# Output projection by seven block products, with the sums of its left operand added by transfers within SBUF

## The chip, the cores and the metric

The kernel runs on one core of a Trainium2 chip. The metric is the time of one execution on the device in microseconds (us); of the kernel before three runs were taken: 902.49, 902.62 and 902.78 us, median 902.62. The engines are named as in the profile: PE (TensorE, the matrix unit), DVE (VectorE), ACT (ScalarE), POOL (GpSimd) and SP (SyncE, which here only issues transfers).

## The reference

One layer of a hybrid backbone: 512 latent tokens and 256 context tokens of width 1024, all arithmetic in float32. What the change touches is the output projection of the token mixer, the residual and the second norm behind it:

```python
merged = sigmoid(ga) * (a @ w_br_a) + sigmoid(gb) * (ob @ w_br_b)   # 512 x 1024
y_x    = merged @ w_o                                              # 512 x 1024 x 1024
x      = x + g1x * y_x
hx2    = rms_norm(x, norm2_g) * (1 + sc2x) + sh2x
x      = x + g2x * conv_ffn(hx2, ...)       # up to 2 x 2816, 3x3 depthwise conv, gelu, down to 1024
```

`g1x`, `sh2x`, `sc2x` and `g2x` are slices of `silu(c) @ w_ada + b_ada`.

## The kernel before

**Products in float32.** Each operand of a large product is split into two float32r tiles: `hi` is the cast on ACT, `lo` the rest by a subtraction on DVE. A product is three matmuls, hi·hi, hi·lo and lo·hi (L423, L441, L1382).

**Weights.** All weights pass as tiles of 128 x 1024 numbers (512 KB) through one list, `specs`. `stream_load` (L250) issues a tile's transfer on SP's queue into one of five `raw` buffers, `stream_split` (L260) makes `wh` on ACT (L277) and `wl` on DVE (L278), five of each, and `weights()` (L300) hands out the next tile, splits two ahead and loads four more ahead.

**Stages, in order of time.** Projections of q, k, v, u with the gated linear attention of four heads between them (to about 248 us); then five products of 512 x 1024 x 1024, for r, vs, ga, gb and w_br_a, each by `gate` (L1387); then w_br_b and w_o by `wide_tm` (L444); the second norm; the up-projection with the convolution (22 pairs of tiles, to 790 us); the down-projection.

**Seven block products.** `gate` and the down-projection split tokens, inner dimension and columns in halves and form the four blocks of a product from seven block products instead of eight (Winograd's form of Strassen's scheme). A block product of a gate is 24 matmuls of 128x128 by 512 columns (`gate_product`, L1373). Sums of quarters of the weights are made in HBM by POOL's transfers, with an add in the transfer where there is a second summand (`sums_build`, L230). Such a transfer is issued behind a certain matmul (`behind_pe`, L106); each call of `weights()` advances the list of these transfers, those of the gates from the first tile on, those of the down-projection from tile `SUMS0` = 90 on. Sums of the left operand are made by DVE.

**The output projection before.** `wide_tm` takes all eight products: per column half and token tile t, 24 matmuls. In the first half the weights are the outer loop, in the second the token tiles. `mg_turn` (L1580) turns one 128-column slice of `merged` by four 128x128 transposes on PE and splits it: four of the eight slices inside the product with w_br_b, four inside that with w_o, by `hook`.

**The gate columns.** `ada2` (L1192) makes four slices of the conditioning in the background, one step per `tick`. At its end a product with a matrix of ones spreads each of four rows over all partitions; for `sh` and `sc` DVE multiplies it with the identity (L1231) and reduces it (L1235), which gives them as columns.

**Behind the output projection.** `wo_add` (L1664) multiplies with `g1` and adds the residual, ACT squares and sums (L1668), `norm2_root` and `norm2_scale` scale a token tile, `norm2_turn` (L1640) turns two token tiles by 16 transposes, and `norm2_out` (L1652) applies `sh` and `sc` on ACT and splits. `turn_first` (L1672) does so for tokens 0 to 255; it stands 27 matmuls before the end of the output projection. The first tile of the up-projection then starts with the columns of these 256 tokens (24 matmuls of 256 columns, and 16 of the second tile), before the other 256 tokens are turned.

**What sets the order.** A scheduler sets the order of each engine's queue, except where `in_order` (L94) or `behind_last` (L391) fix it; from `turn_first` to the first tile of the up-projection the order of PE, ACT and DVE is the order of the code. Within an engine's queue nothing overtakes.

## Time and profile before

| | |
|---|---|
| time, median of three runs | 902.62 us |
| the profiled execution | 904.17 us, its span 902.4 us |
| PE busy | 887.0 us (98%), 4440 matmuls |
| DVE busy | 742.1 us (82%) |
| ACT busy | 482.4 us (53%) |
| POOL busy | 85.3 us (9%) |
| granted clock of PE | 0.997 of full speed |

A page of the profile shows one execution. A matmul's row is longer than its share of the time, since the next one starts before it ends; the distance between two starts counts. In the chain of waits (the work that ended last, followed back) each piece has its start, its length and its line, so that a stretch of PE can be read from it directly.

### The profile page before, as it was taken

How to read it: one execution, taken by the hardware profiler on the slowest of the kernel's cores; microseconds unless marked ns; L12 is line 12 of the kernel's file. 1: busy time of each engine (PE TensorE's matmuls, PEld its weight loads, DVE VectorE, ACT ScalarE, POOL GpSimd, SP SyncE). 2: the span in 40 equal slices, each digit the busy share in tenths (PEclk: the TensorE clock that was granted, in tenths of full speed). 3: DMA queues.
4: the chain of work that ended last, by engine and by line, in shares of the span. 5: the costliest groups of instructions: out<-in, count | busy, mean ns of one | idle time of the engine just before them, and what ended most of it. 6: DMA issues, size and time to landing. Idle time of an engine off the chain costs nothing.

```text
span 902.4 us, 12467 instructions
## 1 busy us (share of the span) xinstructions
PE 887.0 (98%) x4440; PEld 739.4 (82%) x4440; DVE 742.1 (82%) x1227; ACT 482.4 (53%) x799; POOL 85.3 (9%) x134
## 2 busy tenths in 40 slices
PE   7999999999999999999999999999999999999996
PEld 5678888988888888888888889888888888888885
DVE  6468777969789899689998658887899987896996
ACT  6256554848676665767433347433443334366663
POOL 1312222321000000000000010001111110000000
PEclk9999999999999999999999999999999999999998
DMA  9984999999268678777994951998999993256552
GB/s 273 349 281 101 299 277 212 233 328 230 72 206 264 192 260 256 244 233 246 388 336 150 308 164 55 283 306 173 195 212 177 182 191 105 89 162 205 174 185 95
DMA packets 155308, 196.12 MB, mean 217 GB/s; under 512 B 9273, under 2 KB 88453, under 8 KB 155245
## 3 DMA queue, kind: packets, MB, share of 16 engines
q1 hardware_dynamic: 131229, 137.39, 48.0%
q0 software_dynamic: 21024, 52.65, 26.3%
q10 hardware_dynamic: 2992, 5.28, 1.6%
q8 instruction: 35, 0.57, 0.2%
q14 instruction: 28, 0.23, 0.1%
HBM read 186.90 MB, written 58.72 MB: 272 GB/s over the span
## 4 chain that ended last, share of the span: by engine, by line
PE 93%; SPq 2%; DMA 2%; DVE 1%; ACT 1%; issue 0%; ACTq 0%
PE mm L423 34%; PE mm L1382 15%; PE mm L441 11%; PE gl L1863 10%; PE gl L1382 6%; PE gl L959 3%; PE mm L1863 2%; DMA wa<-in_w_ada_dram 2%; PE mm L723 1%; PE mm L1071 1%; PE mm L1121 1%; PE gl L441 1%; SPq L333 1%; PE gl L994 1%; PE gl L1251 1%; SPq L354 1%
## 5 line engine op out<-in xcount | busy, mean ns | idle before, releaser
L277 ACT CAST wh<-raw 128x1024 fp32r<-128x1024 f32 x189 | 195.0, 1037 | 181.3 <-PE mm L423 89.9
L278 DVE TENSOR_TENSOR wl<-raw,wh 128x1024 fp32r<-128x1024 f32 x189 | 225.8, 1200 | 46.4 <-ACT wh L277 46.0
L423 PE MATMUL mm<-h2l,wh 128*128 128x512 f32 (+1 forms) x344 | 133.1, 387 | 0.0
L423 PE MATMUL mm<-h2h,wh 128*128 128x512 f32 (+1 forms) x344 | 133.1, 387 | 0.0
L423 PE MATMUL mm<-h2h,wl 128*128 128x512 f32 (+1 forms) x344 | 133.1, 387 | 0.0
L1715 DVE SCALAR_TENSOR_TENSOR cacc<-ca,ccol,cacc 128x441 f32<-128x441 f32 (+2 forms) x176 | 121.9, 695 | 4.4
L423 PEld LDWEIGHTS mm<-h2l,wh 128*128 128x128 f32 x344 | 64.6, 188 | 13.1
L423 PEld LDWEIGHTS mm<-h2h,wl 128*128 128x128 f32 x344 | 64.6, 188 | 13.1
L423 PEld LDWEIGHTS mm<-h2h,wh 128*128 128x128 f32 x344 | 64.6, 188 | 13.1
L1863 PE MATMUL gl<-wl,dah 128*128 128x512 f32 x132 | 51.4, 389 | 0.0
L1863 PE MATMUL gl<-wh,dah 128*128 128x512 f32 x132 | 51.4, 389 | 0.0
L1863 PE MATMUL gl<-wh,dal 128*128 128x512 f32 x132 | 51.4, 389 | 0.0
L236 POOL DMA_DIRECT2D sum<-in_ffn_w_down_dram x24 | 13.2, 554 | 376.0 <-PE mm L441 257.1
L1212 DVE SCALAR_TENSOR_TENSOR acc<-wa,cs,acc 128x512 f32<-128x512 f32 x64 | 46.3, 746 | 0.0
L1716 ACT ACTIVATE cacc<-cacc 128x512 f32<-128x512 f32 x22 | 13.9, 633 | 59.5 <-DVE cacc L1715 59.4
L1382 PE MATMUL mm<-wh,xs 128*128 128x512 f32 x128 | 41.1, 393 | 0.0
L423 PE MATMUL mm<-hxh,wh 128*128 128x512 f32 x104 | 41.0, 394 | 0.0
L423 PE MATMUL mm<-hxl,wh 128*128 128x512 f32 x104 | 40.7, 391 | 0.0
L423 PE MATMUL mm<-hxh,wl 128*128 128x512 f32 x104 | 40.6, 390 | 0.0
L1382 PE MATMUL mm<-wh,hxh 128*128 128x512 f32 x96 | 37.8, 393 | 0.0
L1382 PE MATMUL mm<-wh,hxl 128*128 128x512 f32 x96 | 37.5, 390 | 0.0
L1382 PE MATMUL mm<-wl,hxh 128*128 128x512 f32 x96 | 37.4, 390 | 0.0
(475 smaller groups left out, 2006.6 us busy)
## 6 DMA issues: line engine op xcount, KB each, us to landing
raw<-in_w_in_dram SPq DMA_DIRECT2D x52, 512.0 KB
wa<-in_w_ada_dram SPq DMA_DIRECT2D x96, 256.0 KB
raw<-sum SPq DMA_DIRECT2D x46, 512.0 KB
raw<-in_ffn_w_up_dram SPq DMA_DIRECT2D x44, 512.0 KB
sum<-in_ffn_w_down_dram POOLq DMA_DIRECT2D x30, 512.0 KB, 6.3
sum<-in_w_in_dram POOLq DMA_DIRECT2D x28, 512.0 KB, 8.6
sum<-sum POOLq DMA_DIRECT2D x22, 512.0 KB, 6.9
raw<-in_ffn_w_down_dram SPq DMA_DIRECT2D x15, 512.0 KB
```

What stands on the lines that cost most here:

```text
L236: behind_pe(lambda: G.dma_start(sums[b][dst], ap), G)
L277: A.copy(wh, raw)
L278: V.tensor_tensor(wl, raw, wh.bitcast(F32), op=ALU.subtract)
L333: dma(t_, w_ada[0, kp * nk * P:(kp + 1) * nk * P, c0:c0 + cg].rearrange("(k p) c -> p k c", p=P))
L423: T.matmul(ps, a[:, k, :], b[:, c0:c0 + n], start=(k == 0 and i == 0), stop=(k == KT - 1 and i == 2))
L441: T.matmul(ps, a[:, t * P:(t + 1) * P], b[:, k % 2, :], start=(k == 0 and i == 0), stop=(k == KT - 1 and i == 2))
L959: T.matmul(ps, p_, q_, start=(start and z == 0), stop=(stop and z == 2))
L1212: behind_last(lambda: V.scalar_tensor_tensor(acc[i], coming.pop(0), cs[:, k, 0:1], acc[i], op0=ALU.mult, op1=ALU.add), V)
L1382: T.matmul(banks[t], a(kk, t), w[:, kk, :], start=(first and b == 0 and kk == 0 and i == 0), stop=(b == 1 and kk == 1 and i == 2), skip_gr ...
L1715: V.scalar_tensor_tensor(o, a_[:, r0 + dy:r1 + dy, c0 + dx:c1 + dx], wcol(tap), o, op0=ALU.mult, op1=ALU.add)
L1716: A.activation(acc, acc, AF.Gelu)
L1863: T.matmul(ps, a, w[:, kk, :], start=(first and kk == 0 and i == 0), stop=(last and kk == n_ - 1 and i == 2), skip_group_check=True)
```

## The change

The product with w_o is taken by seven block products. In detail:

- `w_o` becomes a sixth entry of `gate_weights`: eight sums of two blocks of its quarters are built in HBM by 16 more transfers on POOL's queue, behind those of w_br_a. Its tiles in `specs` are 14 instead of 8, in the order `WO_ORDER` = (0, 3, 1, 2, 5, 4, 6).
- `m_turn` turns a block of `merged` (a11, a12, a21, a22, for each half b of the inner dimension) by four transposes; six of the eight blocks now lie inside the product with w_br_b, two in the first block product. Of the left sums p1, s2, q4, s3 for b = 0, 1, six additions are made by POOL's transfers from one SBUF tile into another with an add (`m_add`), two on DVE; `m_pair` splits them.
- Results leave in another order: column half 0 of tokens 0 to 255, column half 1 of them, then column half 1 of tokens 256 to 511, then column half 0 of those. The two token tiles of a half are normed together. `turn_first` stands behind the first six matmuls of the last block product. PE's order is fixed for the whole stage.
- `sh` and `sc`: ACT copies row 0 of each of the four products with ones and writes it to HBM (`col_rows`, 16 rows of 128), SP reads the 16 rows back, PE turns them, DVE copies the columns.
- The sums of the down-projection begin at tile 106 instead of 90, with one more step at every fourth tile.
- Four of the eight normalisations of `vs` go from DVE to ACT.

```diff
-SUMS0 = 90
+SUMS0 = 106
...
+WO_ORDER = (0, 3, 1, 2, 5, 4, 6)
...
-gate_weights.append((quarters(w_br_a[0], 0), sum_tiles(2)))
+gate_weights += [(quarters(w_[0], 0), sum_tiles(2)) for w_ in (w_br_a, w_o)]
...
-            for _ in range((i >= at and (at > 1 or i < R_AT or gate_pace(i))) + (at <= i < DENSE)):
+            for _ in range((i >= at and (at > 1 or i < R_AT or gate_pace(i))) + (at <= i < DENSE) + (i >= SUMS0 and at > 1 and i % 4 == 0)):
...
+    def cols_load():
+        rows_c = late([16, P], s="rows")
+        dma(rows_c, col_rows)
+        return lambda: columns(rows_c, 16, "col_both", gl)
...
-                t_ = heap([P, 4, P], s="dg")
-                V.tensor_tensor(t_, ps.rearrange("p (b r) -> p b r", b=4),
-                                ident.unsqueeze(1).to_broadcast([P, 4, P]), op=ALU.mult)
-                if kind not in cols:
-                    cols[kind] = const([P, 8], "col_" + kind)
-                V.reduce_sum(cols[kind][:, j * 4:j * 4 + 4], t_, axis=AX.X)
+                t_ = late([1, 512], s="row")
+                A.copy(t_, ps[0:1, :])
+                adma(col_rows[4 * len(rows_out):4 * len(rows_out) + 4].rearrange("(o b) p -> o (b p)", o=1), t_)
+                rows_out.append(kind)
...
+            if not hf:
+                A.activation(z, z, AF.Identity, bias=shift[:, t:t + 1], scale=var[:, t:t + 1])
...
+    def add(dst, src):
+        G.dma_start(dst, src, accum_op=ALU.add)
...
+    def m_pair(name, b, src, sign):
+        hi, lo = heap([P, 2, 256], F32R, s="mh"), late([P, 2, 256], F32R, s="ml")
+        if sign > 0:
+            A.copy(hi, src)
+            V.tensor_tensor(lo, src, hi.bitcast(F32), op=ALU.subtract)
+        else:
+            A.mul(hi, src, -1.0)
+            V.scalar_tensor_tensor(lo, src, -1.0, hi.bitcast(F32), op0=ALU.mult, op1=ALU.subtract)
+        msum[name, b] = hi, lo
+
+    def m_add(name, b):
+        dst, src = {"p1": ("p1", "a22"), "s2": ("p1", "a11"), "q4": ("p1", "n21"), "s3": ("s3", "a11")}[name]
+        add(mraw[dst, b], mraw[src, b])
...
-    wide_tm(ob, brb_done, brb_step, {(2 + j // 2, 4 * (j % 2)): lambda j=j: mg_turn(j) for j in range(4)})
+    wide_tm(ob, brb_done, brb_step, { (1, 0): lambda: m_do("ta110"), (1, 3): lambda: m_do("ta210", "a110"), (1, 6): lambda: m_do("ta120", "+s30"),
+                                    (2, 1): lambda: m_do("ta220", "+p10"), (2, 4): lambda: m_do("ta111"), (2, 6): lambda: m_do("p10", "+s20"),
+                                    (3, 0): lambda: m_do("ta211"), (3, 2): lambda: m_do("a111", "s20", "+q40"), (3, 6): lambda: None})
...
-    wide_tm(mg, wo_done, hook, {(2, 6): turn_first})
+    WO0 = len(traced())
+    wo_product(0, X, True, {(1, 0): lambda: m_do("ta121", "ta221", "p11")})
+    for t in range(2):
+        A.copy(Y[t], X[t])
+    m_do("s30", "q40", "+s31")
+    ada2_cols()
+    wo_product(3, Y)
+    m_do("s21", "+q41", "a220")
+    squares = [wo_add(0, t, Y[t]) for t in range(2)]
+    wo_product(1, Z, True)
+    m5 = [taken(z) for z in Z]
+    for f in squares:
+        f()
+    wo_product(2, X, False, {(1, 0): lambda: taken_out(0)})
+    taken_out(1)
+    m_do("q41", "s31", "a221")
+    crow_turn(0)
+    behind_last(lambda: A.activation(small(1, "root"), eps_t, AF.Sqrt), A)
+    ada2_end()
+    wo_product(5, Z)
+    for t in range(2):
+        wo_out(1, t, Z[t])
+    scaled(2, 0, 1)
+    crow_turn(1)
+    wo_product(4, X)
+    squares = [wo_add(1, t + 2, combine(m5[t], X[t], ALU.subtract)) for t in range(2)]
+    wo_product(6, X, False, {(0, 1): turn_first})
+    for k2 in (2, 3):
+        norm2_out(0, k2, N2[1][k2], A.copy)
+    for t in range(2):
+        squares[t]()
+        wo_out(0, t + 2, X[t])
+    scaled(2, 2, 3)
+    in_order(WO0, T.engine)
```

Where the order moves. First, ACT's queue around the end of the product with w_br_b; `wh` are casts of weights, `acch` of the conditioning's rows, `mgh` of slices of `merged`. Before:

```order
L415 CAST acch_5232<-acc_4240 128x512
L415 CAST acch_5236<-acc_4243 128x512
L415 CAST acch_5240<-acc_4246 128x512
L415 CAST mgh_5253<-gl_5248 128x512
L277 CAST wh_5354<-raw_5108 128x1024
L277 CAST wh_5409<-raw_5111 128x1024
L415 CAST mgh_5274<-gl_5269 128x512
L277 CAST wh_5457<-raw_5118 128x1024
L277 CAST wh_5488<-raw_5358 128x1024
```

Now, at the same place (`mq` are unsplit blocks of `merged`, `mh` and `ml` their splits; `mh_5277` is p1 of block 0, which one of the new transfers fills):

```order
L1615 COPY mq_5252<-gl_5247 128x512
L1615 COPY mq_5269<-gl_5264 128x512
L1623 ACTIVATE mh_5277<-mq_5223 128x512
L420 CAST acch_5287<-acc_4267 128x512
L282 CAST wh_5410<-raw_5131 128x1024
L420 CAST acch_5291<-acc_4270 128x512
L282 CAST wh_5422<-raw_5133 128x1024
L420 CAST acch_5295<-acc_4273 128x512
L282 CAST wh_5428<-raw_5139 128x1024
L1620 CAST mh_5309<-gl_5303 128x512
L282 CAST wh_5492<-raw_5414 128x1024
```

Ahead of the second w_o tile's cast (`wh_5410`) there now stands a copy that waits for a transfer within SBUF.

Second, ACT's queue behind the first w_o tiles. Before:

```order
L415 CAST mgh_5377<-gl_5372 128x512
L277 CAST wh_5492<-raw_5413 128x1024
L415 CAST mgh_5404<-gl_5399 128x512
L415 CAST mgh_5432<-gl_5427 128x512
L277 CAST wh_5523<-raw_5462 128x1024
L415 CAST mgh_5453<-gl_5448 128x512
L277 CAST wh_5527<-raw_5497 128x1024
L277 CAST wh_5557<-raw_5548 128x1024
L1668 ACTIVATE yt_5531,ss_5332<-x_1209_5310 128x512
```

Now:

```order
L1242 COPY row_5361<-gl_5358 1x512
L1608 ACTIVATE mq_5449<-gl_5444 128x512
L1243 DMA col_rows<-row_5361 1x512
L1608 ACTIVATE mq_5450<-gl_5444 128x512
L1615 COPY mq_5458<-gl_5453 128x512
L1768 COPY mm_5408<-mm_5404 128x512
L1768 COPY mm_5409<-mm_5405 128x512
L1623 ACTIVATE mh_5461<-mq_5449 128x512
L1620 CAST mh_5479<-mq_5224 128x512
L1623 ACTIVATE mh_5483<-mq_5223 128x512
L282 CAST wh_5498<-raw_5426 128x1024
L282 CAST wh_5544<-raw_5490 128x1024
```

Between two casts of weights (`wh_5492`, shown above, and `wh_5498`) there now stand 17 other entries, three of them transfers; `mh_5483` is the split of q4 of block 0, the third sum in a row that a transfer makes in the tile `mq_5223`.

Third, DVE's queue ahead of the up-projection: `yt` and `x` are gate and residual, `xs` the scaled tokens, `h2h` and `h2l` the normed ones split for the up-projection. Before:

```order
L1662 TENSOR_TENSOR h2l_5344<-h2f_5709,h2h_5343 128x256
L1661 CAST h2h_5345<-h2f_5716 128x256
L1662 TENSOR_TENSOR h2l_5346<-h2f_5716,h2h_5345 128x256
L1662 TENSOR_TENSOR h2l_5348<-h2f_5716,h2h_5347 128x256
L1631 TENSOR_REDUCE n2s_5724<-ss_5332 128x1
L475 RECIPROCAL rstd_5726<-rstd_5726 128x1
L1666 TENSOR_TENSOR yt_5757<-mm_5732,g_956_4173 128x512
L1667 TENSOR_TENSOR x_1216_5324<-x_1216_5324,yt_5757 128x512
L1636 TENSOR_SCALAR xs_5760<-x_1213_5318,rstd_5726 128x512
L1631 TENSOR_REDUCE n2s_5765<-ss_5332 128x1
L475 RECIPROCAL rstd_5767<-rstd_5767 128x1
L1636 TENSOR_SCALAR xs_5770<-x_1215_5322,rstd_5767 128x512
```

Now:

```order
L1731 TENSOR_TENSOR h2l_5399<-h2f_5826,h2h_5398 128x256
L1730 CAST h2h_5400<-h2f_5833 128x256
L1731 TENSOR_TENSOR h2l_5401<-h2f_5833,h2h_5400 128x256
L1731 TENSOR_TENSOR h2l_5403<-h2f_5833,h2h_5402 128x256
L1735 TENSOR_TENSOR yt_5841<-mm_5404,g_954_4155 128x512
L1736 TENSOR_TENSOR x_1234_5373<-x_1234_5373,yt_5841 128x512
L1735 TENSOR_TENSOR yt_5846<-mm_5405,g_954_4155 128x512
L1736 TENSOR_TENSOR x_1236_5377<-x_1236_5377,yt_5846 128x512
L1750 TENSOR_REDUCE n2s_5850<-ss_5387 128x2
L480 RECIPROCAL rstd_5852<-rstd_5852 128x2
L1705 TENSOR_SCALAR xs_5855<-x_1234_5373,rstd_5852 128x512
L1705 TENSOR_SCALAR xs_5859<-x_1236_5377,rstd_5852 128x512
```

Before, one token tile's gate and residual (`yt_5757`) stood behind the last split of the first 256 tokens (`h2l_5348`); now two stand there, and both tiles wait for one root.

More of the change, by code (lines that the diff above doesn't have):

```diff
@@ L1385, in backbone_kernel, with gate @@
     banks = []
-    def gate(out, pool, at={}, mids=late, quad=r_quad, sum_=r_sum, pool1=None):
+    def gate(out, pool, at={}, mids=late, quad=r_quad, sum_=r_sum, pool1=None, order=GATE_ORDER, during={}):
         pool1 = pool1 or pool
@@ new lines, in m_turn @@
+    def m_turn(name, b):
+        i, hf = int(name[1]) - 1, int(name[2]) - 1
+        ps = gl()
+        for kk in range(2):
+            for t in range(2):
+                o = (2 * kk + t) * P
+                c0 = (2 * i + kk) * P
+                T.transpose(ps[:, o:o + P], sgb_t[b, 2 * hf + t][:, c0:c0 + P], ident)
+        src = ps.rearrange("p (k t) -> p k t", k=2)
+        raw = lambda: heap([P, 2, 256], s="mq")
+        if name == "a12":
+            z = mraw["p1", b], mraw["s3", b] = raw(), raw()
+            for t_ in z:
+                A.mul(t_, src, -1.0)
+        elif name == "a21":
+            mraw["n21", b] = raw()
+            m_pair(name, b, src, 1)
+            A.mul(mraw["n21", b], src, -1.0)
+        else:
+            mraw[name, b] = raw()
+            A.copy(mraw[name, b], src)
@@ new lines, in m_sum, with m_do @@
+    def m_sum(name, b):
+        if b and name in ("p1", "s2"):
+            dst, src = mraw["p1", b], mraw["a22" if name == "p1" else "a11", b]
+            V.tensor_tensor(dst, dst, src, op=ALU.add)
+        m_pair(name, b, mraw["p1" if name in ("s2", "q4") else name, b], -1 if name in ("p1", "s2", "q4") else 1)
+    def m_do(*what):
+        for w_ in what:
+            if w_[0] == "t":
+                m_turn(w_[1:4], int(w_[4]))
+            elif w_[0] == "+":
+                m_add(w_[1:-1], int(w_[-1]))
+            else:
+                behind_last(lambda: m_sum(w_[:-1], int(w_[-1])), V)
@@ L1697, in backbone_kernel, with scaled, wo_out @@
-    hooks += [(lambda j=j: (mg_turn(j), tick(WT[0])),) for j in range(4, 8)] + [(tick, WT[1])] * 4 + [(ada2_end,)]
-    hooks += [(crow_turn, 0), (crow_turn, 1)]
-    wide_tm(mg, wo_done, hook, {(2, 6): turn_first})
+    def scaled(n, *ts):
+        s_ = small(len(ts), "n2s")
+        V.reduce_sum(s_, ss2[:, ts[0]:ts[-1] + 1, :], axis=AX.X)
+        r = rstd_of(s_, len(ts), D)
+        for t in ts:
+            norm2_scale(t, r[:, t - ts[0]:t - ts[0] + 1])
+    def wo_out(hf, t, src):
+        wo_add(hf, t, src)()
@@ new lines, in wo_product @@
+    def wo_product(n, bank_, first=False, during={}):
+        name = ("a11", "p1", "s2", "a21", "s3", "q4", "a22")[n]
+        gate_product(bank_, m_of(name), first, during)
+    X, Z, Y = [[bank() for _ in range(2)] for bank in (mm, gl, mm)]
+    taken_out = lambda t: V.tensor_tensor(Z[t], m5[t], X[t], op=ALU.subtract)
+    WO0 = len(traced())
+    wo_product(0, X, True, {(1, 0): lambda: m_do("ta121", "ta221", "p11")})
+    for t in range(2):
+        A.copy(Y[t], X[t])
+    m_do("s30", "q40", "+s31")
```

112 lines of the change are left out of this document (50 added, 62 removed).

## The prediction

> **What bounds the kernel now.** First the page's busy times and chain, then PE's waits.
>
> ```profile
> PE 887.0 (98%) x4440; PEld 739.4 (82%) x4440; DVE 742.1 (82%) x1227; ACT 482.4 (53%) x799; POOL 85.3 (9%) x134
> PE 93%; SPq 2%; DMA 2%; DVE 1%; ACT 1%; issue 0%; ACTq 0%
> PE mm L487 <- DMA rows<-in_b_ada_dram: 5.9, 1, 5.9
> PE gl L632 <- DMA wa<-in_w_ada_dram: 1.0, 3, 0.4
> ```
>
> PE is the bound, and its waits lie at the start; a matmul that is left out is time won unless PE waits instead. So the question is whether DVE and ACT keep up in the changed stage. The chain of waits there, then the busy times of that stage (by its window) and of the last two gates:
>
> ```profile
> 498.02 0.23 PE gl L1223
> ...
> 502.16 0.44 PE gl L1583 x4
> ...
> 512.66 10.93 PE mm L441 x48
> ...
> 529.03 0.10 PE gl L1621
> ...
> 539.58 1.75 PE gl L1648 x16
> 541.32 6.14 PE mm L441 x27
> 547.46 2.87 PE mm L423 x24
> 550.33 1.92 PE mm L1736 x16
> 552.25 1.75 PE gl L1648 x16
> ```
> ```profile
> core 0: us, PE busy (x) PEld busy (x) DVE busy (x) ACT busy (x) POOL busy (x), PEclk, DMA share, GB/s
> 497.86:547.46 49.60, 49.60 (x237) 41.13 (x236) 31.09 (x58) 21.48 (x42) 4.43 (x8) 1.00 0.65 209
> ```
> ```profile
> 400.00:452.00 52.00, 52.00 (x231) 43.09 (x230) 49.27 (x64) 31.55 (x43) 0.00 (x0) 1.00 0.89 312
> ```
>
> The output projection begins at 498.02 with the conditioning's products and ends at 547.46, PE without a gap at full clock. DVE is busy 31.09 of 49.6 us there. In the gates it is busy 49.27 of 52 us, and PE does not wait: a full DVE alone is no loss, a late one is.
>
> **What PE saves.** A matmul takes 10.93/48 = 0.2277 us. Eight products of 24 become seven: 24 x 0.2277 = **5.46 us** less. Added is one small transposition for the columns, 0.10 (the 529.03 piece). The 32 transpositions of `merged` remain; two groups of 0.44 us move ahead of the stage, which changes no sum. Counted from the stage's start (time 0 below), the new PE work is 8 x 0.23 + 168 x 0.2277 + 2 x 0.44 + 0.3 + 1.75 = 43.0 us; before, 547.46 − 498.02 = 49.4.
>
> **What DVE and ACT get.** Six more weight tiles to split, a rewritten split of twelve left operands, copies between banks. Durations and distances of starts, from the groups of instructions and the timeline:
>
> ```profile
> L278 DVE TENSOR_TENSOR wl<-raw,wh 128x1024 fp32r<-128x1024 f32 x17 | 20.7, 1221 | 8.1 <-ACT wh L277 8.0
> L1636 DVE TENSOR_SCALAR xs<-x,rstd 128x512 f32<-128x512 f32 x4 | 1.9, 487 | 0.1
> ```
> ```profile
> 497.80 1.23 DVE L278 TENSOR_TENSOR wl<-raw,wh 128x1024 fp32r<-128x1024 f32 x1
> 498.94 0.69 DVE L1588 TENSOR_TENSOR dc<-mm,dc 128x512 f32<-128x512 f32 x1
> 499.54 0.68 DVE L1231 TENSOR_TENSOR dg<-gl,ident 128x512 f32<-128x512 f32 x1
> ```
> ```profile
> 490.02 1.67 ACT L415 CAST acch<-acc 128x512 fp32r<-128x512 f32 x3
> 556.33 2.98 ACT L277 CAST wh<-raw 128x1024 fp32r<-128x1024 f32 x3
> 329.78 0.38 ACTq L1242 DMA_DIRECT2D kept<-obf  x1
> ```
>
> So back to back: on DVE 1.14 us for a weight tile and 0.60 for 512 columns; on ACT 0.54 for 512 columns (1.67/3, rounded down for the overlap), 0.97 for a weight tile, 0.36 for a transfer's issue.
>
> ACT's queue from time 0, as the order shows it: `wh_5492` to 1.2, five copies to 3.9, two issues 4.6, one copy 5.1. Then `mq_5449` waits for the eight transpositions inside the first block product (PE: 1.84 + 0.3 + 2.73 + 0.88 = 5.7). With an issue and two copies `mq_5458` is there at 7.5. Y's second copy waits for the first product's end, 8.5, so it ends at 9.1; three splits to 10.8; **`wh_5498` at 11.8**. DVE reached `wl_5493` at 5.7; it must stand still for `mq_5458` (1.8 us), add (0.6), and again for `wh_5498` (3.6 us), since its queue has the rest of that tile next. PE needs it only at 15.3 (8.5 + 24 + 6 matmuls), so PE does not yet wait.
>
> From 11.8 DVE has, up to the splits of the normed tokens: 11 weight tiles (12.5), 25 operations of 512 columns (15.0, and 0.3 as some have a scalar), two scalings (0.8), seven small ones (1.4), together 30.0, so it is through at about 42. Then the twelve splits `h2h`/`h2l`, three per 1.0 us by these rows:
>
> ```profile
> 544.57 0.29 DVE L1661 CAST h2h<-h2f 128x256 fp32r<-128x256 f32 x1
> 544.89 0.76 DVE L1662 TENSOR_TENSOR h2l<-h2f,h2h 128x256 fp32r<-128x256 f32 x2
> 545.57 0.28 DVE L1661 CAST h2h<-h2f 128x256 fp32r<-128x256 f32 x1
> ```
>
> So they end at S = 46.0, and PE's last block product ended at E = 43.3 (43.0 and 0.3 of waiting, below). PE goes on with 24 + 16 short matmuls, 2.87 + 1.92 = 4.79 us, and then needs the second 256 tokens scaled. The end of that chain before:
>
> ```profile
> 547.50 0.69 DVE L1666 TENSOR_TENSOR yt<-mm,g 128x512 f32<-128x512 f32 x1 [0.25 <-PE mm L441]
> 548.22 0.69 DVE L1667 TENSOR_TENSOR x<-x,yt 128x512 f32<-128x512 f32 x1
> ...
> 550.42 0.49 DVE L1636 TENSOR_SCALAR xs<-x,rstd 128x512 f32<-128x512 f32 x1
> ```
>
> From the end of the residual (548.91) to the scaled tile (550.91) it takes 2.0 us, and PE had 1.3 us to spare. Now two tiles' gate and residual (2.6 us) stand behind S in fixed order, so the tiles are scaled at S + 4.6 and S + 5.0, and PE waits S + 4.9 − (E + 4.79) = **2.8 us**.
>
> **The transfers within SBUF** are unseen so far. What stands behind each: ACT's copy `mh_5277` waits for the first one (+p10) with four weight casts behind it; the second (+s20) is issued after `ml_5278`, the third (+q40) after `ml_5325`. Bounds from POOL's transfers, from issue to landing; `fx` goes from SBUF to HBM with 256 KB, `sum` is within HBM and mostly 512 KB:
>
> ```profile
> DMA to landing us min/median/max: 5.1/5.5/6.9
> DMA to landing us min/median/max: 3.1/7.2/14.1
> sum<-sum POOLq DMA_DIRECT2D x2, 256.0 KB, 4.9
> sum<-sum POOLq DMA_DIRECT2D x22, 512.0 KB, 6.9
> ```
>
> I take 4.3 us, between the least of all and the `sum` of equal size, since nothing passes through HBM and the down-projection's sums are out of this stage. +p10 is issued at about −9.8 and lands at −5.5; DVE's own queue reaches `ml_5278` at −4, so its wait is hidden; +q40 lands at 8.6, before ACT's queue gets to it (10.3). PE waits 0.3 us at the fourth row of the conditioning, whose bank ACT frees behind `wh_5492`. At 5.5 us the same walk gives `wh_5410` a microsecond later, 1.5 us of waiting in the first block product, `wh_5498` at 13.0, and behind ACT's wait for +q41 DVE 2.3 us later at S: PE loses 5.2 us in all.
>
> [...]
>
> **The rest.** The 16 sums of w_o take POOL between 220 us and about 345:
>
> ```profile
> 220.37 0.87 POOL L238 DMA_DIRECT2D sum<-sum  x1 [2.55 <-DMA sum<-sum]
> 463.71 0.59 POOL L236 DMA_DIRECT2D sum<-in_ffn_w_down_dram  x1 [242.47 <-PE mm L441]
> 220.00:248.00 28.00, 28.00 (x150) 24.21 (x149) 23.03 (x44) 17.60 (x36) 0.87 (x1) 1.00 0.41 95
> 248.00:292.00 44.00, 44.00 (x195) 36.43 (x195) 39.57 (x53) 30.11 (x42) 0.00 (x0) 1.00 0.74 229
> ```
>
> POOL stood idle there 242 us, and the DMA engines had room (0.41 and 0.74 of their time); they are ready over 100 us before use. I cost them at nothing. The sums of the down-projection, begun later and run 5 steps for 4 tiles, end about where they ended. The columns through HBM: last row written at 16, two transfers in a row, by the bounds above 3.1 to 5.5 us each, needed at 25: between 2.8 us to spare and 2 us of waiting; I take nothing. The four normalisations moved to ACT fall under PE's full queue.
>
> **Sum.** −5.46 + 0.10 + 0.3 + 2.8 = −2.3 us. The profiled execution took 904.17 us, 1.55 more than the median of 902.62, with a span of 902.4; on it the change gives 901.9, on the median **900.3 us**.
>
> **The rivals.**
> *DVE keeps up.* If the 5.4 us for which DVE stands still shrink to 3 or less, S is set by ACT's chain: `turn_first` begins 1.75 + 18 x 0.2277 = 5.85 before E, and ACT takes 1.36 us per pair of slices (541.10 to 542.46 between its casts), so S is about E + 0.8 and PE still waits 0.9: −5.46 + 0.1 + 0.9 = −4.5, 898.1 us. For it: the gates run with DVE full. Against: those have no queue of 17 entries between two weight casts.
>
> ```profile
> 541.10 0.41 ACT L1661 CAST h2h<-h2f 128x256 fp32r<-128x256 f32 x1
> 542.46 0.41 ACT L1661 CAST h2h<-h2f 128x256 fp32r<-128x256 f32 x1
> ```
>
> *The sums land at 5.5 us,* as `fx` did: −5.46 + 0.1 + 5.2 = −0.2, 902.4 us. Against: `fx` ran while the first loads filled the DMA engines.
>
> *Slower: the three sums in a row land at 6.9 us each,* as the 512 KB sums. Each waits for the split of the one before, so beyond 5.5 us a microsecond counts three times in `wh_5498`: 4.2 more, 906.6 us. It decides from 6.2 us on. [...]
>
> *It does not save what it says:* the 16 sums and the loads collide in the gates and PE waits there about what it saves, 902 to 904 us. Against: the room above.
>
> **How the numbers follow.** Forecast 0.45 (899.0 to 901.6), DVE keeps up 0.17, landing at 5.5 us 0.20, slower 0.13, collision 0.05. About 0.2%, 1.8 us, is what a measurement here can tell from no change: 900.8 and 904.4 are the bounds. Two thirds of the forecast (0.30), all of the first rival (0.17) and a part of the second (0.06) give faster 0.53; same 0.31; slower 0.16. The range of 8 in 10 reaches from the first rival to where the slow one begins: 897.8 to 904.5.
>
> **What would show it.** In the profile after: 168 matmuls in the stage; DVE waiting on ACT's `mq` and `wh` near the first block product, some 5 us together; PE's longest wait at the 16 transpositions of the second 256 tokens, 2.8 us, released by DVE's `xs`. A landing of the transfers within SBUF over 5 us, PE waiting at `mh` or `ml` or in the gates, or no wait ahead of the up-projection would make me wrong.

## The result, and the profile after

Nine runs of each kernel: before 902.78 us (902.36 to 904.39), after **905.21 us** (901.40 to 907.74), a ratio of 1.0021 with a 95% interval of 1.0012 to 1.0031. The change costs some 1.9 us where the prediction had it win 2.3, and 905.2 lies 0.7 us above the range. The times also scatter more: their standard deviation is 1.8 us, before 0.7. Three slow executions, of 988, 1806 and 2311 us, are left out of every figure below.

The profiled execution took 905.21 us with a span of 903.4. Its page, busy times and the chain's shares:

```profile
PE 883.4 (98%) x4417; PEld 734.1 (81%) x4417; DVE 747.4 (83%) x1231; ACT 502.1 (56%) x832; POOL 102.9 (11%) x156
PE 38%; issue 3%; DVE 2%; DMA 1%; ACT 1%; POOL 0%; POOLq 0%; DVEq 0%; ACTq 0%
```

PE works 3.6 us less than before (887.0), and yet the span grew: the work went, and waits came. The chain of waits, which was 93% PE before, is followed through PE for only 38% and then leaves it. What PE waited for (engine, line, what it waited for; us in total, times, longest):

```profile
PE mm L492 <- DMA rows<-in_b_ada_dram: 6.0, 1, 6.0
PE gl L1717 <- DVE xs L1705: 2.1, 1, 2.1
PE gl L637 <- DMA wa<-in_w_ada_dram: 1.2, 3, 0.5
PE gl L1395 <- ACT mh L1623: 1.2, 1, 1.2
PE gl L1234 <- ACT mq L1612: 0.5, 1, 0.5
...
PE mm L1395 <- DVE wl L283: 0.3, 1, 0.3
...
PE mm L1395 <- DVE rstd L480: 0.3, 1, 0.3
```

The first and the third stand at the start and were there before. The 2.1 us (`xs`) are the wait that the prediction names, at the transposes of the second 256 tokens. The 0.5 us (`mq`) are the 0.3 that it puts at the fourth row of the conditioning. The 1.2 us (`mh`) is one that it does not have. The chain of waits shows what is behind it:

```profile
519.40 7.58 DMA mq<-mq
...
527.00 0.64 ACT mh L1623
...
528.68 1.28 ACT L1782
...
530.18 0.95 ACT wh L282
...
531.15 1.23 DVE wl L283
```

`mq<-mq` at 519.40 is the last of the six sums within SBUF, +q41. It took **7.6 us** from issue to landing. The timeline of ACT, then that of DVE, in the same stage (start, length, and in brackets the idle time before and what ended it):

```profile
527.00 0.63 ACT L1623 ACTIVATE mh<-mq 128x512 fp32r<-128x512 f32 x1 [4.13 <-DMA mq<-mq]
...
528.68 1.28 ACT L1782 ACT_TABLE_LOAD   x1
```
```profile
506.76 0.69 DVE L1634 TENSOR_TENSOR mq<-mq,mq 128x512 f32<-128x512 f32 x1 [1.61 <-ACT mq L1615]
511.46 2.36 DVE L283 TENSOR_TENSOR wl<-raw,wh 128x1024 fp32r<-128x1024 f32 x2 [4.00 <-ACT wh L282]
...
527.67 0.69 DVE L1624 SCALAR_TENSOR_TENSOR ml<-mq,mh 128x512 fp32r<-128x512 f32 x1 [2.08 <-ACT mh L1623]
...
531.15 1.23 DVE L283 TENSOR_TENSOR wl<-raw,wh 128x1024 fp32r<-128x1024 f32 x1 [1.33 <-ACT wh L282]
...
548.08 0.68 DVE L1735 TENSOR_TENSOR yt<-mm,g 128x512 f32<-128x512 f32 x1
```

DVE stands still four times, not twice: 1.61 and 4.00 us as predicted (1.8 and 3.6), then 2.08 behind +q41, then 1.33 because ACT loads the table of the square root (1.28 us) ahead of the next weight cast. So the splits of the first tokens end at 548.08.

To compare kernels I cut the span at four rows that all of them have: the first product of the projections, of the gates, the first with w_br_a, and the first matmul of the second tile of the up-projection behind the second 256 tokens. The stage from the third to the fourth holds the products with w_br_a, w_br_b and w_o and the second norm, and is where the change is; the rest of the span stays (347.6 us before, 347.5 after). Three more profiles serve for scale: the changed kernel again, and the kernel before twice more.

| kernel | first product starts | projections | gates | stage of the change | span |
|---|---|---|---|---|---|
| before | 91.8 | 156.2 | 166.3 | 140.5 | 902.4 |
| before, second profile | 90.1 | 156.3 | 166.2 | 140.5 | 900.8 |
| before, third profile | 90.6 | 156.3 | 166.2 | 140.5 | 901.3 |
| after | 91.7 | 156.2 | 166.7 | **141.3** | 903.4 |
| after, second profile | 91.4 | 156.2 | 166.1 | **138.1** | 899.3 |

Two things are to be explained: why the stage takes 141.3 us in one execution of the changed kernel and 138.1 in another (before it stays within 0.1), and why before mostly starts a microsecond earlier than after.

### The profile page after: what moved, and what is told of

Same layout as the page of the kernel before. It is cut to its first block, busy times and chain, and to the rows that moved or that the text cites. A ratio compares the mean times of both kernels' runs of the same rounds, so it can differ in the third digit from the quotient of the medians.

```text
span 903.4 us, 12530 instructions
## 1 busy us (share of the span) xinstructions
PE 883.4 (98%) x4417; PEld 734.1 (81%) x4417; DVE 747.4 (83%) x1231; ACT 502.1 (56%) x832; POOL 102.9 (11%) x156
## 5 line engine op out<-in xcount | busy, mean ns | idle before, releaser
L282 ACT CAST wh<-raw 128x1024 fp32r<-128x1024 f32 x196 | 201.5, 1038 | 171.4 <-PE mm L428 89.9
L283 DVE TENSOR_TENSOR wl<-raw,wh 128x1024 fp32r<-128x1024 f32 x196 | 233.9, 1200 | 48.3 <-ACT wh L282 47.6
L243 POOL DMA_DIRECT2D sum<-sum x28 | 24.8, 909 | 111.9 <-PE mm L1395 39.1
```

What stands on the lines that cost most here:

```text
L243: behind_pe(lambda: G.dma_start(sums[b][dst], ap, accum_op=ALU.add), G)
L282: A.copy(wh, raw)
L283: V.tensor_tensor(wl, raw, wh.bitcast(F32), op=ALU.subtract)
```

## The experiments

Where an entry of DVE's or ACT's queue is moved, the order of both engines from the product with w_br_b on was first written out as the changed kernel has it, so that nothing else moves; it shifts line numbers by about 10. The table load alone was moved without that, and in its profile all other entries of DVE and ACT in the stage stand as in the changed kernel. Each ratio is to the kernel before, timed on the same chip.

### Are the late sums the cause?

Two of the six sums, +s31 and +q41, landed late (7.8 and 7.6 us), the other four in 3.2 to 3.8 us in all twelve profiles, but for one of 4.5 and one of 4.3. The first three in after, and +s31 (count, KB, median us from issue to landing):

```profile
mq<-mq POOLq DMA_DIRECT2D x3, 256.0 KB, 3.3
```
```profile
mq<-mq POOLq DMA_DIRECT2D x1, 256.0 KB, 7.8
```

**First**, DVE adds those two itself.

```diff
-        add(mraw[dst, b], mraw[src, b])
+        add(mraw[dst, b], mraw[src, b], (name, b) in ON_DVE)   # {("s3", 1), ("q4", 1)}: V.tensor_tensor
```

> The sums +s31 and +q41 are additions on DVE instead of transfers; every other instruction keeps its place on its engine. Theory A (DVE reaches the end of the stage late, because ACT's mh_5622 waits 4.1 us for +q41, which took 7.6 us to land, and because the table load of 1.28 us stands behind that wait): ACT makes mh_5622 at about 523.3 instead of 527.0 and loads its table before DVE needs the next weight cast, so DVE's waits of 2.08 and 1.33 us go and two additions of 0.60 us come, S is 2.2 us earlier, PE's wait ahead of the transpositions of the second 256 tokens shrinks from 2.1 us to under 0.5, the wait of 1.2 us at mh to about 0.5: 2.5 to 3 us less than the changed kernel, about 902.4 beside a kernel before of 902.8, with less scatter from run to run. Theory B (the time is lost to the extra traffic of the sixteen w_o sums in the gates, and so does the scatter come from there): within 0.6 us of the changed kernel, 904.6 to 905.8, same scatter.

Measured: 1.0007 (0.9999 to 1.0016), stage 138.9 us. The stage is 2.4 us shorter than after's, with 1.2 us more work on DVE.

**Second**, the two are left out.

```diff
-        add(mraw[dst, b], mraw[src, b])
+        if (name, b) not in (("s3", 1), ("q4", 1)):
+            add(mraw[dst, b], mraw[src, b])
```

> The transfers +s31 and +q41 are left out, so two of the left operands lack a summand and the output projection's values are not the reference's; every other instruction stands where the changed kernel has it. This is the price of the two landings with nothing put in their place. Theory A: ACT reaches mh_5622 at about 523.3 (it waited there 4.1 us), DVE's waits of 2.08 and 1.33 us go, the stage takes 138 to 138.5 us instead of 141.3, and the kernel 2.5 to 3 us less than the changed kernel beside it. Against the 138.9 us of the kernel that put two DVE additions in their place, the 1.2 us of the additions would then be mostly visible or hidden. If landing is not the cause (a chain of DVE's own work), under 1 us is won.

Measured: **0.9988** (0.9980 to 0.9997), stage 137.6 us. So the late sums hold some 2.5 us of time, from 1.0016 (same chip) or 1.0021 to 0.9988: without them, two left operands lacking a summand, the kernel is faster than before. PE's waits in that stage are then only these:

```profile
PE gl L1729 <- DVE xs L1717: 1.2, 1, 1.2
...
PE gl L1244 <- ACT mq L1622: 0.5, 1, 0.5
```

**Third**, +s31 is issued at 506.55, among eight loads of `x` on SP (2 MB, issued from 505.65 to 510.17, two of them ahead of it); here these go earlier.

```diff
-(2, 4): lambda: m_do("ta111")
+(2, 4): lambda: (x_load(), m_do("ta111"))
```

> The eight loads of x (256 KB each) stand on SP's queue ahead of two loads of w_o sums instead of behind four weight loads; order on PE, DVE, ACT and POOL is that of the changed kernel. In the changed kernel four sums within SBUF landed in 3.3 to 3.6 us while the DMA engines were busy 0.3 to 0.8 of their time, and +s31 and +q41 in 7.8 and 7.6 us while they were busy 0.9 to 1.07 with these loads. Theory A, with the landing set by the traffic it runs beside: +s31 and +q41 land in 3.5 to 5 us, ACT makes mh_5622 at about 523 to 524.5, and 2 to 3 us are won, 902.2 to 903.2 beside 902.8. [...]

Measured: 1.0014 (1.0004 to 1.0025). +s31 landed in 4.9 us instead of 7.8, so it was the loads that held it up. The time did not follow, for ACT is not yet at its reader by then. +q41 took 5.9 us, PE no longer waited at `mh`; but the stage took 141.2 us all the same, for a reason that comes under the clock below.

### Is it the order around the wait?

**The table load.** ACT's root table is fetched in front of the split that waits for +q41, while ACT stands idle anyway.

```diff
+    behind_last(lambda: A.activation(small(1, "root"), eps_t, AF.Sqrt), A)
     wo_product(2, X, False, {(1, 0): lambda: taken_out(0)})
     taken_out(1)
     m_do("q41", "s31", "a221")
     crow_turn(0)
-    behind_last(lambda: A.activation(small(1, "root"), eps_t, AF.Sqrt), A)
```

> The small square root that loads ACT's table (1.28 us, then 0.20 us) goes ahead of mh_5622, where ACT stood idle 4.1 us for +q41. Nothing else moves on any engine. Theory A: DVE's wait of 1.33 us at the next weight cast goes, S is 1.3 us earlier, PE waits 0.8 us instead of 2.1 at the transpositions of the second 256 tokens: 1.3 us less than the changed kernel, about 903.9 beside 902.8. Theory B (traffic in the gates): no difference, 905.2 plus or minus 0.6.

Measured: 0.9995 (0.9987 to 1.0004), stage 138.1 us although +q41 took 5.9. Level with before, and 1.9 to 2.3 us better than after (1.0016 and 1.0021), more than the 1.28 us that the load takes; how that comes about is not shown by itself, but none of its eleven executions has the low clock that is treated below.

**The splits of the left operand.** While DVE waits 4.00 us for `wh_5498`, three splits stand behind the two weight tiles though ACT has written their other half already.

```diff
 DVE's queue:
+ml_5462<-mq,mh   ml_5480<-mq,mh   ml_5484<-mq,mh
 wl_5499<-raw,wh  wl_5545<-raw,wh
-ml_5462<-mq,mh   ml_5480<-mq,mh   ml_5484<-mq,mh
```

> On DVE alone, the three splits ml_5462, ml_5480 and ml_5484 stand ahead of the weight tiles wl_5499 and wl_5545 instead of behind them; all other orders as in the changed kernel. ACT has their upper halves ready at 509.5 to 510.4, while DVE stood still 4.0 us for the cast wh_5498. Theory A (every microsecond by which DVE is late at the end of the stage costs PE one): 1.8 us of that wait are filled, everything behind is 1.4 to 1.8 us earlier, the transfer +q41 too: PE waits about 0.5 instead of 2.1 us at the second 256 tokens, 903.5 beside 902.8. If the end is set by +q41's landing at an hour of its own (the loads beside it, not its issue), DVE only waits longer for mh_5622 and 0.5 us or less is won.

Measured: **0.9987** (0.9978 to 0.9996), stage 137.5 us: the wait is filled with 1.8 us of work that was due anyway.

**Both**, and then both with the normalisations of `vs` back on DVE (all eight, as before the change):

> The root ahead of mh_5622 and the three splits ml ahead of two weight tiles, both together, the orders otherwise as in the changed kernel. Alone they took 2.7 and 3.7 us off against the kernel before on their chip. Theory A: they fill different waits of DVE (1.33 us at a weight cast behind the table load; 1.8 of the 4.0 us at wh_5498), so DVE ends its splits about 3 us earlier than in the changed kernel, and PE's wait ahead of the second 256 tokens goes to 0.5 us or less: 900 to 901 beside 902.5, faster than both kernels. If one gain hides the other, 901.2.

> As the one before, and the four normalisations on DVE again. Theories A and D together: 0.3 to 1 us less than that kernel, 899.5 to 900.3 beside 902.5. Theory A alone: the same as that kernel.

Measured: 0.9987 (0.9978 to 0.9996) and **0.9970** (0.9959 to 0.9982). The last is the fastest kernel found, 900.2 us against 903.3 on its chip: it beats both. That the normalisations are worth 1.3 us more on top, though they lie 200 us ahead of the stage, is the next question. PE's two waits for the stage and the one at the start in that kernel:

```profile
PE gl L1723 <- DVE xs L1711: 1.1, 1, 1.1
PE gl L1244 <- ACT mq L1617: 0.5, 1, 0.5
...
PE gl L647 <- DMA wa<-in_w_ada_dram: 0.2, 1, 0.2
```

**Four more moves** on top: one copy ahead of the last cast before the stage, the scalings ahead of a weight tile on both engines, one weight tile behind the last splits, and `turn_first` six matmuls sooner.

```diff
-    wo_product(6, X, False, {(0, 1): turn_first})
+    wo_product(6, X, False, {(0, 0): turn_first})
```

> The fastest kernel so far (root early, left splits first, normalisations on DVE; stage 137.5 us) with four moves more: ACT copies mq_5308 ahead of the cast wh_5492, so that PE's wait of 0.67 us at the fourth conditioning row goes; the scaling of the first 256 tokens stands ahead of a weight tile on DVE and on ACT; DVE splits the up-projection's second weight tile behind the normed tokens; PE transposes the first 256 tokens six matmuls earlier. Theory A (what is left in the stage is 0.7 us there and 1.2 to 1.4 us ahead of the second 256 tokens): 0.7 to 1.7 us less than that kernel, ratio 0.995 to 0.9965 of the kernel before, 898.7 to 899.8 beside 902.8.

Measured: 0.9972 (0.9961 to 0.9983), stage 137.8 us. Nothing gained: a miss.

### The parts outside the stage

**The normalisations back on DVE,** alone:

```diff
-            if not hf:
-                A.activation(z, z, AF.Identity, bias=shift[:, t:t + 1], scale=var[:, t:t + 1])
-            else:
-                V.tensor_scalar(z, z, mv[:, t, 0:1], var[:, t:t + 1], op0=ALU.subtract, op1=ALU.mult)
+            V.tensor_scalar(z, z, mv[:, t, 0:1], var[:, t:t + 1], op0=ALU.subtract, op1=ALU.mult)
```

> The four normalisations of the gate's values that the change gave to ACT are on DVE again, as before; the orders of the output projection's stage are those of the changed kernel. In the changed kernel and in two of the experiments so far PE lost 0.3 to 0.9 us near 337 to 345 us at a weight's lower half: ACT had its table load (1.28 us), var, a copy and the four normalisations (2.2 us) ahead of the cast that this split waits for. Theory D (these four cost PE time, as they stand ahead of a weight cast that is late in some executions because its load competes with the w_o sums): that wait is gone, 0.3 to 1 us less than the changed kernel, 904.2 to 904.9 beside 902.8 (903.9 to 904.6 beside 902.5). Theory A alone (only the stage of the output projection loses): no difference, and the wait at 337 to 345 us moves to another instruction or was chance.

Measured: 1.0015 (1.0006 to 1.0024). The first product starts at 90.5 (after 91.7), but +q41 lands in 8.9 us, PE waits 2.5 us at `mh`, and the stage takes 142.6. What is won at the start is lost there.

**The other way round:** the kernel before, given the 16 sums of w_o in HBM (unused), then those and the four normalisations on ACT (twice), then the normalisations alone.

```diff
-HERE = (2,3,1,4,0)
+HERE = (2,3,1,4,0,0)
-    gate_weights.append((quarters(w_br_a[0], 0), sum_tiles(2)))
+    gate_weights += [(quarters(w_[0], 0), sum_tiles(2)) for w_ in (w_br_a, w_o)]
...
+    shift = const([P, 4], "shift")
+    V.scalar_tensor_tensor(shift, mv[:, :, 0], -1.0, var, op0=ALU.mult, op1=ALU.mult)
...
+            if not hf:
+                A.activation(z, z, AF.Identity, bias=shift[:, t:t + 1], scale=var[:, t:t + 1])
```

> The kernel before, and beside it the sixteen transfers that build the w_o sums, at the places on POOL's queue at which the change has them; nothing reads the sums, all else is the kernel before. Theory B (their traffic costs time in the gates by itself): 1 us or more slower than the kernel before, with more scatter. Theory A, and D as the combination of both (the traffic alone delays some loads, but without the normalisations on ACT the casts still come in time): within 0.5 us of the kernel before.

> The kernel before with two parts of the change: the sixteen w_o sums built and not used, and the four normalisations on ACT. The sums alone made no difference (1.0001, gates 166.2 us). Theory D (normalisations on ACT stand ahead of weight casts whose loads the sums delay): the gates take 166.5 to 168 us in the profile, with a wait of PE at 335 to 346 us, and the time is 0.4 to 1.5 us above the kernel before. Theory A alone: no difference, 166.1 to 166.4 us in the gates.

> The kernel before with the sums unused and the normalisations on ACT once more, on this chip. Timed, it was 1.2 us above the kernel before (1.0014), but its profiled execution lost nothing in the gates (166.1 us). Theory D: again 0.5 to 1.5 us above, and a second profile may show PE waiting at 335 to 346 us. If the first result was chance: within 0.4 us.

> The kernel before with one part of the change alone: the four normalisations on ACT, no w_o sums. Theory D as a matter of ACT's order alone: 0.5 to 1.2 us above the kernel before, as with the sums. Theory D as the combination with the delayed loads: within 0.4 us of it. If the four cost nothing in either kernel: within 0.4 us here, and the repeat of the combination beside it too.

Measured: the sums alone 1.0001 (0.9993 to 1.0010); both together 1.0014 (1.0005 to 1.0023) and 1.0025 (1.0016 to 1.0034); the normalisations alone **1.0018** (1.0009 to 1.0027). The sums cost nothing. The normalisations alone cost 1.6 us (1.3 and 2.3 with the sums), and not where they run, which is where Theory D puts it: projections, gates and stage are as before (156.3, 166.1, 140.5), while the first product starts at 92.4 instead of 90.1 to 91.8.

So something acts before 92 us that is issued after 200. The four normalisations bring one new constant tile, `shift`, of 16 bytes a partition. It takes 32 and moves all tiles of the three large pools (weights, `heap`, `late`): they began at multiples of 512 bytes, and now begin 32 past one (the first `raw` tile at byte 23040 of a partition before, at 23072 with `shift`). The traffic of the first 50 us tells such kernels apart; the line of the transfers, of the kernel before (second profile) and with the normalisations alone (second profile):

```profile
DMA packets 19497, 16.09 MB, mean 322 GB/s; under 512 B 2299, under 2 KB 16747, under 8 KB 19493
```
```profile
DMA packets 18437, 15.23 MB, mean 305 GB/s; under 512 B 1632, under 2 KB 15975, under 8 KB 18433
```

and PE's wait for the conditioning's weights in the same two:

```profile
PE gl L632 <- DMA wa<-in_w_ada_dram: 0.3, 1, 0.3
```
```profile
PE gl L632 <- DMA wa<-in_w_ada_dram: 1.5, 4, 0.5
```

In all twelve profiles with the shifted tiles the first 50 us move 301 to 309 GB/s, in all eight without 317 to 322. The start follows less sharply: 91.2 to 93.0 us with the shift and 90.1 to 91.8 without, on the mean 1.2 us apart. Three single profiles among these, the kernel before twice and the normalisations alone:

> The kernel before, once more, for a second profiled execution. Its times form two groups, 901.5 to 902.5 and 903.2 to 904.2; the first profile belongs to the upper one. The profiles of this kernel and of its variants with the sums or the normalisations agree to 0.2 us in every stretch behind the first 92 us and differ only in these, 91.3 to 92.4. Theory E (the two groups are two lengths of the start, in which PE waits for loads): a profile of the lower group has 90.2 to 90.8 us to that point, and the same 156.2, 166.3, 140.5 and 347.6 behind it. If a lower profile has a shorter stretch elsewhere, that stretch is where the normalisations cost time.

> As the run before, a third profile of the kernel before. Theory E: the time follows the length of the first stretch alone.

> The kernel before with the normalisations on ACT, a second profile. All twelve timed executions were in the upper group (903.56 to 905.60). Theory E: its first stretch is 91.5 us or more again, and the gates take 166.1 us, so the 1.6 us that it lost against the kernel before are no wait behind these four instructions. Theory D: the gates take over 166.8 us.

They came out at 902.49 and 903.00 us, starting at 90.1 and 90.6, and at 904.37, starting at 92.1. Behind the start nothing differs from the first profiles by more than 0.1 us, as Theory E has it; why the start of the kernel before itself varies from 90.1 to 91.8 is open.

**Addresses alone:** the changed kernel with `shift` stretched to 512 bytes, so that only addresses change (the first `raw` tile at byte 23552, a multiple of 512).

```diff
-    shift = const([P, 4], "shift")
+    shift = const([P, 128], "shift")[:, :4]
```

> The changed kernel whole, every instruction in its place on every engine, with one line different: the small tile shift, 16 bytes on a partition, is given 512 bytes. In the changed kernel and in all kernels with the normalisations on ACT this tile moves every tile behind it by 32 bytes, so that they begin 32 bytes past a multiple of 512, where before they began on one; here they begin on one again. Theory F (loads into tiles that are 32 bytes off are slower): the first 50 us move 317 to 322 GB/s as in the kernels without that tile, not 301 to 307; PE waits 0.2 to 1.0 us for wa instead of 1.2 to 1.5; the first stretch takes 90.2 to 91.8 us; 1.2 to 1.7 us less than the changed kernel, so within 0.6 us of the kernel before, 1.0000 plus or minus 0.0007, the rest being the late stage. Theory D (the four instructions themselves): no difference to the changed kernel, 1.0012 to 1.0031. The stage of the output projection itself is not expected to change: 138 to 143 us, by how late +q41 lands.

Measured: 320 GB/s, no wait for `wa` at all, first product at 90.4: so rate and start come back with the addresses alone, in one profile. But the time is 1.0018 (1.0007 to 1.0028), no better than after, and the expectation of 1.0000 was missed: in its profile +q41 landed in 8.2 us and the stage took 141.8. That aligning pays in this kernel as it stands is therefore not shown. With the stage mended a gain of 1.3 us shows, 0.9970 against 0.9987 above (same chip), but the normalisations' engine is changed with it there. The kernel before with shifted tiles and nothing else was not run.

### What decides when +q41 lands

The changed kernel again:

> The changed kernel once more, on this chip, beside the three others of this group. Theory A: its stage of the output projection (from the first product of the second branch at 414 us to the second up-projection tile at 555 us in the first profile, 141.3 us against 140.5 before) takes 140.5 to 143 us, according to how late +q41 lands; the gates ahead of it (166.7 against 166.3) 166.1 to 168. Time 1.0012 to 1.0031 of the kernel before.

Measured: 1.0016 (1.0004 to 1.0028), times from 900.87 to 906.77. The profiled execution was one of the shortest: stage 138.1 us, 2.4 less than before, as forecast. Here +q41 landed in 4.4 us. POOL's and SP's queues side by side, first of after, then of this profile (each the issue of +q41, and SP's next two loads):

```profile
519.40 0.87 POOL L1589 DMA_DIRECT2D mq<-mq  x1 [11.98 <-DVE ml L1624]
```
```profile
518.96 0.32 SPq L1200 DMA_DIRECT2D rows<-col_rows  x1
519.38 0.88 SPq L261 DMA_DIRECT2D raw<-sum  x2
```
```profile
518.43 0.87 POOL L1589 DMA_DIRECT2D mq<-mq  x1 [11.98 <-DMA raw<-sum]
```
```profile
518.67 0.32 SPq L1200 DMA_DIRECT2D rows<-col_rows  x1
519.09 0.88 SPq L261 DMA_DIRECT2D raw<-sum  x2
```

and the landings (KB, us from issue to landing), after first:

```profile
mq<-mq POOLq DMA_DIRECT2D x1, 256.0 KB, 7.6
```
```profile
mq<-mq POOLq DMA_DIRECT2D x1, 256.0 KB, 4.4
```

SP issues two loads of 512 KB at nearly the same moment. With those 0.02 us ahead, the sum took 7.6 us; 0.66 us behind, 4.4. (The releaser in brackets is inferred; what +q41 waits for is said below.) The other profiles in which the two loads leave together:

| kernel | +q41 ahead of SP's two loads by, us | lands in, us | stage, us |
|---|---|---|---|
| normalisations on DVE | −0.37 | 8.9 | 142.6 |
| after, addresses aligned | −0.20 | 8.2 | 141.8 |
| after | −0.02 | 7.6 | 141.3 |
| table load early | 0.29 | 5.9 | 138.1 |
| after, second profile | 0.66 | 4.4 | 138.1 |
| splits first | 1.00 | 4.7 | 137.5 |
| table load and splits | 0.52 | 4.6 | 137.6 |
| those, normalisations on DVE | 0.56 | 5.3 | 137.5 |
| those, four more moves | 1.12 | 4.8 | 137.8 |

What stands ahead of the two loads on SP is `rows<-col_rows`, the columns' way back from HBM: SP waits there for ACT's rows to have landed (2.1 us in after), and so the loads leave when those land. POOL's add leaves when DVE has split s2, whose tile it overwrites: 0.3 us behind that split's end in both profiles (519.40 behind 519.11, 518.43 behind 518.13). Two chains that know nothing of one another end within about a microsecond, and what comes first differs from execution to execution. (In the last four rows a third load follows, 1.5 to 2.4 us behind the sum's issue.) No run moved +q41 or these two loads alone, so this is read off nine profiles; the run with `x` early is the one in which loads were moved away from a sum, and +s31 then landed 2.9 us sooner. The bytes that passed while a sum was under way go the same way as the table: up to 0.5 MB, its own included, with landings in 3.2 to 3.4 us, 0.6 to 1.4 MB with 3.3 to 5.9, 1.8 to 2.3 MB with 7.6 to 8.9.

### A wait of 2.1 us, and a granted clock of 0.72 behind it

The stage with `x` early took 141.2 us though PE waited less than in after. The busy times by window around the wait for `xs`, of that kernel and then of after (columns: window, length, busy time of PE, weight loads, DVE, ACT, POOL, granted clock, share of the DMA engines, GB/s):

```profile
544.00:550.00 6.00, 4.48 (x38) 4.28 (x36) 4.68 (x13) 2.85 (x10) 0.00 (x0) 1.00 0.63 170
550.00:556.00 6.00, 5.40 (x32) 5.24 (x32) 4.55 (x14) 5.81 (x11) 0.00 (x0) 0.72 0.01 3
```
```profile
550.00:556.00 6.00, 3.88 (x33) 3.52 (x32) 3.47 (x11) 5.35 (x14) 0.00 (x0) 1.00 0.04 9
556.00:562.00 6.00, 6.00 (x51) 5.96 (x50) 5.79 (x14) 5.04 (x8) 0.00 (x0) 1.00 0.00 0
```

Both waited 2.1 us. In the first the granted clock then fell to 0.72 over 6 us, 1.7 us of work lost; in the second it stayed at 1.00. In the kernel with the normalisations on DVE, around 2.5 us of waiting at `mh`:

```profile
524.00:528.00 4.00, 2.13 (x10) 1.21 (x8) 1.25 (x2) 0.02 (x1) 0.00 (x0) 1.00 1.12 302
528.00:532.00 4.00, 3.34 (x8) 2.43 (x9) 2.16 (x5) 3.97 (x7) 0.00 (x0) 0.64 0.12 34
532.00:536.00 4.00, 4.00 (x18) 3.15 (x18) 3.88 (x7) 3.29 (x5) 0.82 (x2) 0.94 0.32 97
```

Both falls are of the same size: 6 × 0.28 = 1.68 us of work in the first, 4 × 0.36 + 4 × 0.06 = 1.68 in the second. Both come behind the wait: up to 550 and up to 528 us, where PE stood idle already, the clock is 1.00, and PE resumed at 550.6 and at 528.7. In the first the eight matmuls of 256 columns from 553.52 on start 0.21 us apart on the mean (the next one at 555.17), from there on 0.12. The ten other profiles of changed kernels show 1.00 in every window from 520 to 568 us; the 2.1 us in after and a wait as long with the addresses aligned brought no fall. The profiled executions with a fall have a mean clock of 0.996, the eighteen others 0.997 to 0.999.

The mean granted clock, which every run records, shows how often. A loss of 1.7 in 903 us is 0.002 of it. The mean is 0.997 to 0.999 in all 133 counted executions of the kernel before that were timed beside the experiments. It is 0.996 in 8 of 21 executions of after, 6 of 12 with the addresses aligned, 5 of 11 with `x` early, 4 of 11 with the normalisations on DVE, and once in 69 executions of the seven kernels in which +q41 lands early, is made by DVE or is left out. The runs of the second timing of after with 0.997 or less took 905.4 us on the mean, those above 903.1. So the late sum costs the wait, and in many executions the clock too; 8 of 21 times 1.7 us would be 0.6 us on the mean, an estimate. With `x` early it is the wait for `xs` alone that goes before the fall. Why one wait of 2.1 us is followed by a fall and another is not, no run shows.

## Why the prediction was wrong

**What PE saves: right.** The stage has 536 matmuls of 512 columns instead of 560, at the same distance of 0.227 us. By the prediction's terms it would take 140.5 − 5.46 + 0.10 = 135.1 us without waits. It took 138.1 in the second profile (3.0 us lost; the prediction has 3.1; the rows of waits show 2.2 of it) and 141.3 in the first (6.2).

**What DVE and ACT get: right but for one entry.** The waits of 1.61 and 4.00 us stand where they were put, with 1.8 and 3.6. Left out was the table load, L1782, 1.28 us in ACT's queue: it stands behind the late split, so that DVE waits once more, 1.33 us. Moved, it is worth 1.9 to 2.3 us in time. In the second profile, where +q41 landed in 4.4 us, DVE's splits end at S = 45.7 us (forecast 46.0) and the last block product at E = 44.0 (43.3): with the landing as priced, the walk through the queues comes out.

**The wait ahead of the second 256 tokens: right in place and nearly in size,** 2.1 us in one profile, 1.7 in the other, where 2.8 was put. In the first that is in part luck, for S and E are both late by about as much: S at 548.08 − 499.12 = 49.0 us, not 46.0, and the last block product ends at 46.8, not 43.3.

**The step that failed: "The transfers within SBUF", "I take 4.3 us".** One price was taken for six transfers, and the sum has no term for a late one. Four landed sooner (3.3 to 3.6 in after), and there it made no difference; +s31 landed in 7.8 and was covered; +q41 landed in 7.6, and ACT's wait of 4.13 us for it, DVE's of 2.08 and PE's of 1.2 behind it are what the forecast lacks. In the nine profiles of the table it takes 4.4 to 8.9 us. The 5.5 us of `fx` had been set aside because `fx` ran while the first loads filled the DMA engines (busy 0.99 of the first 50 us before), and 4.3 was taken because the sums of the down-projection were gone from the stage. But SP's loads fill them here too: they were busy for 0.91 of the time in which +q41 was under way, and the prediction's own row for the stage before had 0.65 on the mean. SP's queue was not asked. The bound of 6.9 from the sums in HBM was nearer, but I used it for three sums in a row at the stage's start, which landed in 3.3 to 3.6. So the slower rival named about the right price at the wrong place. How busy DVE was beside a sum did not decide: beside +q41 DVE ran the same instructions in both profiles of after, without a pause in the second, and the landings were 7.6 and 4.4 us. The first sum ran beside a DVE that was busy for 3.36 of 3.40 us and landed in 3.3 us; +s31 ran beside one that stood idle for 4.00 us and landed in 7.8. The window of the first:

```profile
487.60:491.00 3.40, 3.40 (x20) 2.79 (x19) 3.36 (x6) 0.86 (x2) 1.77 (x2) 1.00 0.44 77
```

The least landing measured for any of these sums is 3.2 us.

**"The rest", at nothing: half right.** The 16 sums of w_o cost nothing in time (1.0001). Six of the twelve profiles of the changed kernels lose 0.5 to 1.7 us in the gates, near 340 us, and the three of the kernel before with the sums nothing. The collision of the rival it is not, since the last of these sums had landed by 296 us; what it is stays open. The columns through HBM do not make PE wait, but they set the moment at which SP's loads meet +q41. The normalisations were costed by where they run; their price, 1.6 us in the kernel before, lies at the start of the program and most likely came through the tiles' addresses.

**The base.** The profiled execution of before started its first product at 91.8 us, as after does; later ones started at 90.1 and 90.6. So the comparison of the two profiles first shown hides the start.

**The sum, by runs.** From the forecast of −2.3 us to the measured +1.9 are 4.2 us: about 2.5 for the late sums and the clock that they cost in some executions (left out: 1.0021 or 1.0016 to 0.9988), and about 1.6 for the addresses (1.0018 in the kernel before). The second term is carried over from the kernel before: the changed kernel with its addresses aligned was no faster in time, so that its share there is argued and not shown. It closes from the other end too: without the late sums the stage is 2.9 us shorter than before, the start 1.6 longer, together −1.3; measured −1.1.

## What to carry to other kernels

Here the landing of one transfer of 256 KB ran from 3.2 to 8.9 us and went with what was issued in the same microsecond on other queues, so list the loads of all queues around its issue before taking a price from rows of a quiet stretch; where two chains end close together, take the landing with and without the other's bytes, and let one of the two be moved so that the order is certain. A wait between two in-order engines is best filled with work that is ready (three splits and one table load moved, and the normalisations back on DVE, so that the addresses stay as before, made this change worth 2.7 us). When a kernel's start differs though the edit is far from it, compare the transfer rate there and the addresses of the tiles.

## What was not expected of the hardware

- With the tiles 32 bytes past a multiple of 512 the transfers of the first 50 us moved 301 to 309 GB/s, with the tiles at multiples of 512 they moved 317 to 322 (twelve and eight profiles, no overlap). That the addresses lower the rate is shown in one profile, in which stretching the one new tile to 512 bytes brings 320 back; by what mechanism, and how much time it costs by itself, is not shown.
- A 256 KB sum from one SBUF tile into another landed in 3.2 to 3.4 us with little beside it (up to 0.5 MB passing, its own bytes included), in 4.4 to 5.9 when 1 MB of loads was issued 0.3 to 1.1 us behind it, and in 7.6 to 8.9 when they were issued with it or up to 0.4 us ahead.
- A wait of 2.1 us on PE was followed by a granted clock of 0.72 over 6 us in one execution and by 1.00 in two others; one of 2.5 us was followed by 0.64 and 0.94 over 4 us each. The fall took 1.7 us of work both times.
